# Feature-major inputs, tile-major weights, and a start K tile by K tile, in a one-core hybrid encoder layer

## The chip, the core and the metric

The kernel runs on one core of a Trainium2 chip. The metric is the device time of one execution in microseconds (us). Layout work that the host does on arrays before or after the launch is not in it. Engines: PE is TensorE, DVE VectorE, ACT ScalarE, POOL GpSimd, SP the engine whose queue issues every DMA here.

## What is computed

One layer over 512 prompt tokens and 64 sample tokens, 1,024 features, all float32. Cut to what matters here:

```python
h = rmsnorm(x, norm_mix)                    # over the 1024 features
proj = h @ w_in                             # 1024 x 4104, three head groups
# A: short conv + SiLU, L2-normed q/k, gated delta rule in chunks, gate
# B: differential attention (two softmax maps a head), returns its k and v too
# C: trailing means over 2/4/8/16 frames, a 128x128 map a group
x = x + concat(A, B, C) @ w_out             # 1536 x 1024
u = causal_dwconv(rmsnorm(x, norm_ffn) @ ffn_up)     # 1024 x 5632
x = x + (silu(gate) * value) @ ffn_down     # 2816 x 1024
y = rmsnorm(x, norm_final)
```

Besides y it returns the last rows of every convolution and pooling buffer, attention's keys and values, and the delta-rule states.

## The kernel before

The 576 tokens are the columns of every product and the features its partitions. A product (`gemm`) makes 128 output features: for each of 8 K tiles the weight is split in two float32r parts, `w_hi` (ACT, L177) and `w_lo` (DVE, L178), the activation is in two parts as well, and PE runs hi·hi, hi·lo and lo·hi for token columns 0 to 255 and 256 to 575 (`PARTS`): 48 matmuls of 256 or 320 columns. A weight tile comes through `fetch_weight` (L167, SP queue) into `w_raw`, two buffers; `w_hi` and `w_lo` have two each, and `load_weight` runs one or two products ahead. In `w_in` a weight tile is a set of 128 columns: each row of 512 bytes is a piece of its own, 16,416 bytes from the next.

PE runs in the order of the code: `mm` and `transpose` keep it. One stream of products is woven with chains of small work (`spawn`, `yield` of the expected wait), so a small matmul whose operand is late holds up the products behind it. The other engines' order is set by a scheduler when the program is built.

**Start.** x and the parameters come token-major (`load_rows` L297, `prow`). PE first runs 14 products that nobody reads (`keep_warm`), then transposes x into PSUM, 128x128 at a time (`spread`, 40 transposes, and 4 for the parameters); `split` (L347 on ACT, L348 on DVE) makes the two parts `hmix`, and copies (`xs`) go out to a DRAM tensor `xT_d` (L406), from which the residual is read back (L1154). `first_products` runs the first two products by token part. `rstd1`, the scale of each token, is made meanwhile: squares on ACT, a power on POOL, diagonals `dg` on DVE, and PE spreads them over partitions (`over_tokens`).

**Decay chain.** `decay_products` (32 matmuls with `wab`) follow the first two products; `decays` turns them on DVE, ACT and POOL into `gt` (from `y` L498 to L523), PE sums it, `grow` goes to DRAM (`gsum_d`, L535) and comes back as a broadcast `XT` (L607) for `front`, one head's part of the delta rule: PE transposes k, q and v into PSUM banks, ACT squares and scales them (L610, L628), and PE goes on with `kq` products in the banks that come free.

**Later places.** `blk` (L646, L660) and `inv` (L673, L700) are round trips through DRAM around the 32x32 inversions (L669, L671 on DVE); `levels` (`Xc`, `Y`, `XT`) are small matmuls after them. `token_major` transposes each head's keys and values on PE (10 transposes) and stores both; the cached keys `ckr` are transposed as well (4 a head), and `store_rows` (`rows_out`) transposes six small outputs.

Of the kernel before, what the change touches and what calls it, by code (L numbers as in the profile page):

```python
# [15 lines left out]
P = 128  # L16
# [9 lines left out]
WARM = (10, 0, 4)  # L26
# [33 lines left out]
def hybrid_step(ctx: ExitStack, tc: tile.TileContext, I, O):  # L60
# [10 lines left out]
    # The tensor engine runs in the order of the code.  One stream of products is woven with chains of  # L71
    # smaller work: a chain yields how long its next operands take, and the stream fills that time.
# [61 lines left out]

    def weight_sources():
        for h in range(HEADS):
            for t in (4 + h, h, 8 + h):
                yield [w_in[:, t * P:(t + 1) * P]]
        for base in (1536, 3592):
            for h in range(HEADS):  # L140
                yield [w_in[:, base + h * P:base + (h + 1) * P]]
        for h in range(HEADS):
            for base in (2568, 2056, 3080):
                yield [w_in[:, base + h * P:base + (h + 1) * P]]
        for m in range(KT):
# [25 lines left out]
    def split_weight(raw, step=8):  # L171
# [3 lines left out]
        for a in range(0, kt, step):  # L175
            r = slice(a, min(a + step, kt))
            nc.scalar.copy(hi[:, r], raw[:, r])  # L177
            last_split[0] = nc.vector.tensor_sub(lo[:, r], raw[:, r], hi[:, r].bitcast(F32)).ins  # L178
        return [(hi[:, k], lo[:, k]) for k in range(kt)]
# [8 lines left out]
    def weights():  # L188
        """Those of the next product; the ones after them are set going"""
# [21 lines left out]
    def accumulate(ps, ws, xs, start, stop):  # L211
        """Some K tiles of a product"""
# [7 lines left out]
    def gemm_part(ps, ws, xs, k, r):  # L220
        """What one K tile adds to some columns of a product"""
# [4 lines left out]
    def over_tokens(out, r5, pool, stacked=None):  # L226
        """A number per token (tokens on partitions) to all partitions (tokens on columns)"""
# [18 lines left out]
    # ---------------------------------------------------------------- constants and parameters  # L246
# [25 lines left out]
    xT_d = dram.tile([P, KT, T], F32, name="xT_d")  # L272
# [18 lines left out]
    tiles = ((0, P), (P, P), (2 * P, P), (3 * P, P), (NP, NS))  # L291
    xt = [sp.tile([P, D], F32, name=f"x{t}") for t in range(5)]
    prow = sp.tile([P, 4, P], F32, name="prow")

    def load_rows(t):
        t0, n = tiles[t]
        nc.sync.dma_start(xt[t][:n], I["x_prompt"][t0:t0 + n] if t0 < NP else I["x_sample"])  # L297

    nc.sync.dma_start(ident, I["consts"][:, :P])
    load_rows(0)  # L300
    params = I["params"].rearrange("(g p) c -> p g c", p=P)
    nc.sync.dma_start(prow[:, 0], params[:, 0])
    load_rows(1)
    first_raw = [fetch_weight(), fetch_weight()]
    for t in (2, 3, 4):
        load_rows(t)
    nc.sync.dma_start(prow[:, 1:], params[:, 1:])
    nc.sync.dma_start(wab_raw, w_in[:, 2048:2056].rearrange("(k p) m -> p k m", p=P))
    nc.sync.dma_start(cst[:, P:], I["consts"][:, P:])
# [3 lines left out]
    def keep_warm(n):  # L313
        """Products that nobody reads: the tensor engine's clock halves when it idles"""
# [3 lines left out]
    keep_warm(WARM[0])  # L318
    transpose(pg[:, :P], prow[:, 0], ident)
    nc.vector.tensor_copy(par[:, :P], pg[:, :P])  # L320

    def later_parameters():
        ps = bank()
        for g in range(1, 4):
            transpose(ps[:, g * P:(g + 1) * P], prow[:, g], ident)
        nc.scalar.copy(par[:, P:], ps[:, P:512])

    rstd1 = const.tile([P, T], F32, name="rstd1")
    xs = sp.tile([P, KT, T], F32, name="xs")
# [4 lines left out]
    last_hi, last_lo = [None], [None]  # L334

    def spread(ps, k, ts):
        """Features on partitions"""
        t0 = tiles[ts[0]][0] // CUT * CUT
        for t in ts:
            a, n = tiles[t]  # L340
            transpose(ps[:, a - t0:a - t0 + n], xt[t][:n, k * P:(k + 1) * P], ident[:n, :n])

    def split(ps, k, r):
        """Scaled, in two parts"""
        ps = ps[:, :r.stop - r.start]
        hi, lo = hmix[k]
        last_hi[0] = nc.scalar.activation(hi[:, r], ps, AF.Identity, scale=col("norm_mix", k)).ins  # L347
        last_lo[0] = nc.vector.scalar_tensor_tensor(lo[:, r], ps, col("norm_mix", k), hi[:, r].bitcast(F32),  # L348
                                                    op0=ALU.mult, op1=ALU.subtract).ins

    def mean_square(t):
        n = tiles[t][1]
        junk = sp.tile([P, D], F32, name="junk")
        nc.scalar.activation(junk[:n], xt[t][:n], AF.Square, scale=D ** -0.5, accum_out=r5[:n, t:t + 1])

    def first_products():
        """The first two products begin with the tokens that come first"""
        ra, rb = PARTS
        w = [split_weight(first_raw[0], 4)]
        pair = [bank() for _ in range(4)]  # L360
        for t in (0, 1):
            for k in range(KT):
                spread(pair[k // 2][:, k % 2 * CUT:], k, (t,))
            if t == 0:
                mean_square(0)
                keep_warm(WARM[1])
        keep_warm(WARM[2])
        for k in range(KT):
            split(pair[k // 2][:, k % 2 * CUT:], k, ra)
        with tc.issue_after(last_hi[0]), tc.issue_after(last_lo[0]):  # L370
            w.append(split_weight(first_raw[1], 4))
            for j in range(4):
                src = pair[j].rearrange("p (k t) -> p k t", k=2)
                if j >= 2:
                    with tc.issue_after(last_split[0]):
                        nc.vector.tensor_copy(xs[:, 2 * j:2 * j + 2, ra], src)
                else:
                    nc.scalar.copy(xs[:, 2 * j:2 * j + 2, ra], src)
        ps = [psg.tile([P, 1024], F32, name="g") for _ in range(2)]
        for k in (0, 2, 4, 6, 1, 3, 5, 7):  # L380
            gemm_part(ps[0], w[0], hmix, k, ra)
        rows = {}

        def second(k):
            rows[k] = bank()
            spread(rows[k], k, (2, 3, 4))
            split(rows[k], k, rb)
            if k % 2:
                nc.vector.tensor_copy(xs[:, k, rb], rows[k][:, :rb.stop - rb.start])
            else:  # L390
                nc.scalar.copy(xs[:, k, rb], rows[k][:, :rb.stop - rb.start])

        with tc.issue_after(last_hi[0]):
            for t in range(1, 5):
                mean_square(t)
        rsqrt(r5, r5, EPS)
        scale = over_tokens(rstd1, r5, sp, qscale[:, 4:5])
        for k in range(KT):
            gemm_part(ps[1], w[1], hmix, k, ra)
            if k in (4, 5, 6):  # L400
                second(k - 4)
        for k in range(KT):
            gemm_part(ps[0], w[0], hmix, k, rb)
            if k + 3 < KT:
                second(k + 3)
        nc.sync.dma_start(xT_d, xs)  # L406
        with tc.issue_after(last_lo[0]):
            next(scale)
            nc.vector.tensor_scalar_mul(ah, par[:, oq:oq + 60], 0.5)
        for k in range(KT):  # L410
            gemm_part(ps[1], w[1], hmix, k, rb)
            if k == 1:
                later_parameters()
            if k == 3:
                next(scale, None)
                yield ps[0]
        load_weight()
        yield ps[1]
# [7 lines left out]
    # ---------------------------------------------------------------- small tables  # L426
# [19 lines left out]
    # ---------------------------------------------------------------- decay and beta, token-major  # L446
# [14 lines left out]
    def decay_products():  # L461
# [930 lines left out]
```

## Time and profile before

| | us |
|---|---|
| median of 3 runs | 881.69 |
| lowest and highest run | 881.03, 882.58 |
| span of the profiled execution | 886.6 |
| PE busy in it | 855.8 |
| DVE, ACT, POOL busy | 536.6, 367.1, 112.2 |
| bytes moved by DMA | 87.19 MB, mean 98 GB/s |

The profiled execution has its span alone as its time: 886.6 us from the first to the last instruction, 4.9 us more than the median of the runs. A row of a timeline has the start, the duration, engine, line, operation, out<-in with shapes, how many instructions were merged, and in brackets how long the engine had been idle and what ended that. A float32 matmul of `keep_warm` counts twice (x20 is 10). [...]

### The profile page before, as it was taken

The page shows a single profiled execution, that of the slowest core. Times are in us where ns is not written, and L with a number is a line of the kernel's source. Part 1 is how long each engine was busy: PE and PEld are TensorE (multiplying, and loading weights), DVE is VectorE, ACT ScalarE, POOL GpSimd, SP SyncE. Part 2 cuts the span into 40 slices and gives each one's busy share as a digit, 9 for nine tenths or more (in the row PEclk, how much of TensorE's full clock was granted, in tenths as well). Part 3 has the DMA queues.
Part 4 walks back from the last instruction along what each step waited for, and adds up shares of the span by engine and source line. Part 5 has one row for each costly group of instructions (what it writes and reads, how often), then busy time and mean ns, then how long its engine had stood idle before and what let it go on. Part 6 is the DMA issues. An engine that isn't in the chain of part 4 may idle for free.

```text
span 886.6 us, 16175 instructions
## 1 busy us (share of the span) xinstructions
PE 855.8 (97%) x6422; PEld 825.7 (93%) x6422; DVE 536.6 (61%) x1201; ACT 367.1 (41%) x822; POOL 112.2 (13%) x184
## 2 busy tenths in 40 slices
PE   6997989999999999999999999999999999999996
PEld 6887989898999988888999999999999999999996
DVE  3766866597234667667667677767776774323322
ACT  4535655114345455455445343434343432322322
POOL 0141311031000100000001121212121210000001
PEclk7998999997999999999999999999999999999998
DMA  7635544344333633433752323232323232332412
GB/s 200 168 67 106 61 73 73 69 97 91 63 55 43 145 111 97 122 104 100 258 175 72 96 72 96 73 96 72 95 73 96 72 89 74 113 103 79 121 56 106
DMA packets 144901, 87.19 MB, mean 98 GB/s; under 512 B 10247, under 2 KB 137355, under 8 KB 144699
## 3 DMA queue, kind: packets, MB, share of 16 engines
q1 hardware_dynamic: 144826, 86.17, 38.2%
q8 instruction: 50, 0.82, 0.4%
q14 instruction: 25, 0.20, 0.1%
HBM read 72.98 MB, written 13.17 MB: 97 GB/s over the span
## 4 chain that ended last, share of the span: by engine, by line
PE 82%; DMA 8%; DVE 5%; ACT 2%; issue 1%; POOL 1%; SPq 1%; POOLq 0%; DVEq 0%; ACTq 0%
PE g L85 67%; PE m L85 11%; PE m L89 3%; DMA w_raw<-in_w_in_dram 3%; DVE w_lo L178 1%; DMA w_raw<-in_ffn_down_dram 1%; DVE kq L669 1%; DVE kq L671 1%; DMA gsum_d<-grow 1%; DMA blk<-U 1%; DMA inv<-kq 1%; ACT w_hi L177 1%; DMA XT<-gsum_d 1%; SPq L646 0%; DMA a<-blk 0%
## 5 line engine op out<-in xcount | busy, mean ns | idle before, releaser
L85 PE MATMUL g<-wide,w_hi 128*128 128x256 f32 (+1 forms) x1472 | 277.3, 308 | 7.7 <-ACT w_hi L177 6.4
L85 PE MATMUL g<-t,w_hi 128*128 128x256 f32 (+1 forms) x1408 | 242.7, 294 | 0.0
L85 PEld LDWEIGHTS g<-wide,w_hi 128*128 128x128 f32 x1472 | 230.5, 196 | 12.2 <-ACT w_hi L177 6.8
L85 PEld LDWEIGHTS g<-t,w_hi 128*128 128x128 f32 x1408 | 210.2, 188 | 0.0
L177 ACT CAST w_hi<-w_raw 128x1024 fp32r<-128x1024 f32 (+2 forms) x113 | 112.9, 1000 | 170.1 <-PE g L85 132.1
L85 PE MATMUL g<-wide,w_lo 128*128 128x256 f32 (+1 forms) x736 | 167.9, 307 | 1.2 <-DVE w_lo L178 1.2
L178 DVE TENSOR_TENSOR w_lo<-w_raw,w_hi 128x1024 fp32r<-128x1024 f32 (+2 forms) x113 | 130.7, 1158 | 55.3 <-ACT w_hi L177 54.4
L85 PE MATMUL g<-t,w_lo 128*128 128x256 f32 x704 | 150.4, 295 | 0.0
L85 PEld LDWEIGHTS g<-wide,w_lo 128*128 128x128 f32 x736 | 128.8, 196 | 3.6 <-DVE w_lo L178 1.9
L85 PEld LDWEIGHTS g<-t,w_lo 128*128 128x128 f32 x704 | 117.4, 188 | 0.1
L1275 DVE SCALAR_TENSOR_TENSOR c<-u,par,c 128x511 f32<-128x511 f32 (+3 forms) x176 | 78.9, 511 | 2.5 <-ACT c L1271 2.5
L1278 POOL COPY fout<-u 128x4 f32<-128x4 f32 x44 | 51.1, 1161 | 223.2 <-DVE u L1269 223.2
L1269 DVE TENSOR_TENSOR u<-g,rstd 128x576 f32<-128x576 f32 x44 | 33.3, 758 | 59.8 <-PE g L85 58.3
L85 PE MATMUL g<-w,w_hi 128*128 128x256 f32 (+1 forms) x280 | 48.4, 295 | 0.0
L85 PEld LDWEIGHTS g<-w,w_hi 128*128 128x128 f32 x280 | 42.0, 188 | 0.0
L1271 ACT ACTIVATE c<-u,par 128x576 f32<-128x576 f32 x44 | 38.3, 870 | 4.3 <-DVE u L1269 1.4
L1295 ACT ACTIVATE s<-c 128x576 f32<-128x576 f32 x22 | 15.1, 687 | 46.0 <-DVE c L1277 45.9
L270 POOL TENSOR_TENSOR osc<-sso,mhalf 128x5 f32<-128x5 f32 x8 | 9.3, 1168 | 192.5 <-DVE sso L1030 128.9
L85 PE MATMUL g<-w,w_lo 128*128 128x256 f32 (+1 forms) x140 | 29.9, 295 | 0.0
L1205 ACT ACTIVATE junk<-m 128x128 f32<-128x128 f32 (+1 forms) x40 | 10.8, 273 | 44.2 <-PE m L89 35.9
L1206 DVE TENSOR_TENSOR t<-m,nf 128x128 f32<-128x128 f32 (+1 forms) x40 | 11.2, 289 | 22.6 <-ACT junk L1205 22.6
L998 ACT ACTIVATE p<-m,stat,qscale 128x512 f32<-128x512 f32 (+3 forms) x32 | 19.5, 613 | 12.3 <-DVE stat L995 12.3
(336 smaller groups left out, 1061.4 us busy)
## 6 DMA issues: line engine op xcount, KB each, us to landing
w_raw<-in_ffn_up_dram SPq DMA_DIRECT2D x44, 512.0 KB, 3.9
w_raw<-in_w_in_dram SPq DMA_DIRECT2D x32, 512.0 KB, 8.4
w_raw<-in_ffn_down_dram SPq DMA_DIRECT2D x16, 512.0 KB, 4.0
w_raw<-in_w_out_dram SPq DMA_DIRECT2D x24, 256.0 KB, 3.5
w_raw<-in_ffn_down_dram SPq DMA_DIRECT2D x8, 384.0 KB, 3.3
xT_d<-xs SPq DMA_DIRECT2D x1, 2304.0 KB, 8.0
xr<-xT_d SPq DMA_DIRECT2D x8, 288.0 KB, 3.9
x_d<-xr SPq DMA_DIRECT2D x8, 288.0 KB, 2.5
```

Source lines behind the costliest of these rows:

```text
L85: ordered(nc.tensor.matmul(out, lhsT=lhsT, rhs=rhs, start=start, stop=stop), n / 2.4 if rhs.dtype == F32R else max(54, n / 0.6))
L89: ordered(nc.tensor.transpose(out=out, in_=in_, identity=identity), 107)
L177: nc.scalar.copy(hi[:, r], raw[:, r])
L178: last_split[0] = nc.vector.tensor_sub(lo[:, r], raw[:, r], hi[:, r].bitcast(F32)).ins
L998: nc.scalar.activation(p_m[:, :nk], maps[m], AF.Exp, scale=qscale[:, j:j + 1], bias=st[:, m:m + 1], accum_out=st[:, 2 + m:3 + m])
L1205: nc.scalar.activation(junk[:n], src, AF.Square, scale=D ** -0.5, accum_out=op["part"][:n, c, m:m + 1])
L1206: nc.vector.tensor_mul(op["yt"][c][m // 4][:n, (m % 4) * P:(m % 4 + 1) * P], src, op["nf"][:n, m * P:(m + 1) * P])
L1269: nc.vector.tensor_mul(u, ps[:, O0:O1], rstd)
L1271: nc.scalar.activation(c, u, AF.Identity, scale=fw[:, 2, t:t + 1], bias=col("ffn_conv_b", t))
L1275: nc.vector.scalar_tensor_tensor(c[:, a + d:b], u[:, a:b - d], fw[:, j, t:t + 1], c[:, a + d:b], op0=ALU.mult, op1=ALU.add)
L1278: nc.gpsimd.tensor_copy(fout[:, :, :, t], u[:, NP - 64:].rearrange("p (s c) -> p s c", c=64)[:, :, 62:])
L1295: nc.scalar.activation(s, cv[0], AF.Silu)
```

## The change

The host now hands over x feature-major (`xT`, 128 partitions x 8 K tiles x 576), each weight by output tile (a tile's 8 K tiles lie together on a partition, 4,096 bytes in one piece; `w_out` with its K tiles in the order of use), `cache_k` transposed, and takes keys, conv, pool and ffn rows feature-major. So 86 PE transposes go: 40 of x, 4 of parameters, 20 of keys, 16 of cached keys, 6 of `store_rows`; so do the copies behind them and `xT_d`. Values keep their transposes, y stays token-major.

The first two products go K tile by K tile: weights arrive in K tiles 0 to 1 and 2 to 7, x in four pieces of two K tiles; each K tile is split from SBUF over all 576 columns and both products' matmuls for it follow. The sum of squares is now made on ACT and DVE from the pieces (squared in place) and summed over partitions by PE (`token_sums`, after the decay products), so that `rstd1` starts later. `keep_warm` runs 24 products.

```diff
-WARM = (10, 0, 4)
+WARM = 24
...
             for t in (4 + h, h, 8 + h):
-                yield [w_in[:, t * P:(t + 1) * P]]
+                yield w_in[t]
...
-        kt = 0
-        for src in next(sources):
-            n = src.shape[0] // P
-            nc.sync.dma_start(raw[:, kt:kt + n], src.rearrange("(k p) m -> p k m", p=P))
-            kt += n
+        src = next(sources)
+        kt = src.shape[1]
+        nc.sync.dma_start(raw[:, :kt], src)
         return raw[:, :kt]
...
+    nc.sync.dma_start(par[:, :P], I["params"][:, :P])
+    load_first(slice(0, 2))
+    nc.sync.dma_start(xs[0], I["xT"][:, 0:2])
+    load_first(slice(2, 8))
+    for j in range(1, KT // 2):
+        nc.sync.dma_start(xs[j], I["xT"][:, 2 * j:2 * j + 2])
...
+        for j in range(KT // 2):
+            if j < 2:
+                split_first((slice(0, 2), slice(2, 8))[j])
+            for k in (2 * j, 2 * j + 1):
+                x = xs[j][:, k % 2]
+                hi, lo = hmix[k]
+                nc.scalar.activation(hi, x, AF.Identity, scale=col("norm_mix", k))
+                last_lo[0] = nc.vector.scalar_tensor_tensor(lo, x, col("norm_mix", k), hi.bitcast(F32),
+                                                            op0=ALU.mult, op1=ALU.subtract).ins
+                for w in range(2):
+                    for i, (a, b) in enumerate(((his, hi), (his, lo), (los, hi))):
+                        for r in PARTS:
+                            mm(ps[w][:, O0:O1][:, r], a[w][:, k], b[:, r], start=k + i == 0,
+                               stop=k == KT - 1 and i == 2)
+
+            flat = xs[j].rearrange("p k t -> p (k t)")
+            nc.scalar.activation(flat, flat, AF.Square)
+            sq.append(xs[j])
+            nc.vector.tensor_add(xs[j][:, 0], xs[j][:, 0], xs[j][:, 1])
+            if j:
+                nc.vector.tensor_add(xs[0][:, 0], xs[0][:, 0], xs[j][:, 0])
+        with tc.issue_after(last_lo[0]):
+            nc.vector.tensor_scalar_mul(ah, par[:, oq:oq + 60], 0.5)
+            ab_ps = decay_products()
+        token_sums(xs[0][:, 0], r5)
         scale = over_tokens(rstd1, r5, sp, qscale[:, 4:5])
...
+        next(scale)
         load_weight()
+        next(scale, None)
+        yield ps[0]
+        spawn(decays(decay_rows(ab_ps)), 3250)
+        lambdas()
         yield ps[1]
...
-                nc.sync.dma_start(xr, xT_d[:, m])
+                nc.sync.dma_start(xr, I["xT"][:, m])
```

**What moves, on PE behind the first two products.** Before, `dg,ones` (the scale spread over partitions) stands among the second product's matmuls on the later tokens:

```order
L85 MATMUL g<-wide,w_hi 128x320 x2
L85 MATMUL g<-wide,w_lo 128x320
L85 MATMUL m<-dg,ones 128x128 x4
L85 MATMUL m<-dg,ones 128x64
L85 MATMUL m<-r_129,cst 64x1 x2
L85 MATMUL g<-wide,w_hi 128x320 x2
L85 MATMUL g<-wide,w_lo 128x320
```

Now it stands behind the decay products (`wab`) and right behind the sums over partitions that it is made from:

```order
L85 MATMUL m<-wide,wab 128x320
L85 MATMUL m<-ones,x_92 128x1 x4
L85 MATMUL m<-ones,x_92 64x1
L85 MATMUL m<-dg,ones 128x128 x4
L85 MATMUL m<-dg,ones 128x64
L85 MATMUL m<-r_137,cst 64x1 x2
L85 MATMUL g<-wide,w_hi 128x256
```

No product stands any more between the sums and the scale, nor between the scale and the third product, which takes the PSUM buffer that the scaled first product leaves.

**What moves, on DVE between the decay products and `y`,** the first step of the decay chain (`tmp` is a product times `rstd1`, `kq` the conv of a product, `abT` the scaled decay products). Before:

```order
L473 TENSOR_TENSOR abT<-m,rstd_127 40x256
L473 TENSOR_TENSOR abT<-m,rstd_127 40x320
L578 SCALAR_TENSOR_TENSOR kq<-tmp,ah,kq 128x579
L583 SCALAR_TENSOR_TENSOR kq<-tmp,kq 128x579
L578 SCALAR_TENSOR_TENSOR kq<-tmp,ah,kq 128x579
L498 TENSOR_TENSOR y<-m,vec 128x20
```

Now (the 512-column `tmp` of the first product stands directly ahead of it):

```order
L436 TENSOR_TENSOR abT<-m,rstd_136 40x256
L241 COPY qscale<-m 128x1
L530 TENSOR_TENSOR tmp<-g,rstd_136 128x64
L436 TENSOR_TENSOR abT<-m,rstd_136 40x320
L529 TENSOR_TENSOR tmp<-g,rstd_136 128x512
L530 TENSOR_TENSOR tmp<-g,rstd_136 128x64
L449 TENSOR_SCALAR qneg<-qscale 128x5
L534 SCALAR_TENSOR_TENSOR kq<-tmp,ah,kq 128x579
L450 TENSOR_SCALAR qscale<-qscale 128x5
L534 SCALAR_TENSOR_TENSOR kq<-tmp,ah,kq 128x579 x5
L539 SCALAR_TENSOR_TENSOR kq<-tmp,kq 128x579 x2
L461 TENSOR_TENSOR y<-m,vec 128x20
```

Both convs, eight wide instructions, now stand ahead of `y`; before, three of the eight did between `abT` and `y`, and most of the rest lay ahead of `abT`.

**What moves, on SP's queue at the start.** Now the first issues are:

```order
L298 DMA par<-in_params_dram 128x128
L296 DMA w_raw<-in_w_in_dram 128x256 x2
L300 DMA x_92<-in_xT_dram 128x1152
L296 DMA w_raw<-in_w_in_dram 128x768 x2
L303 DMA x_93<-in_xT_dram 128x1152
L303 DMA x_94<-in_xT_dram 128x1152
L303 DMA x_95<-in_xT_dram 128x1152
```

Two of five x tiles, the identity and the first parameters stood ahead of the first weights; now three quarters of x stand behind them. Behind the start both kernels have the same order on PE up to the inversion, and the same eight weight loads ahead of `gsum_d` and `XT`.

## Rows read from the trace of the kernel before

**Rows 1.** The page's busy times: us, share of the span, instructions.
```profile
PE 855.8 (97%) x6422; PEld 825.7 (93%) x6422; DVE 536.6 (61%) x1201; ACT 367.1 (41%) x822; POOL 112.2 (13%) x184
```
**Rows 2.** Waits: who waited for whom, us in total, times, longest.
```profile
PE m L89 <- ACT kt L610: 2.9, 1, 2.9
PE m L85 <- DVE gt L523: 1.7, 1, 1.7
PE g L85 <- DVE a L1117: 1.3, 1, 1.3
...
PE m L85 <- DMA Xc<-inv: 1.1, 2, 0.7
...
ACT w_hi L177 <- DMA w_raw<-in_w_in_dram: 23.2, 6, 8.0
```
**Rows 3.** Windows: stretch and length, busy by engine (instructions), PEclk, DMA share, GB/s.
```profile
3.00:6.00 3.00, 2.56 (x18) 2.40 (x18) 0.22 (x1) 0.91 (x1) 0.00 (x0) 1.00 0.95 349
9.00:10.50 1.50, 0.00 (x0) 0.00 (x0) 0.58 (x2) 0.00 (x0) 0.00 (x0) 1.00 0.56 74
78.00:84.00 6.00, 6.00 (x26) 5.58 (x27) 5.22 (x11) 2.81 (x10) 0.87 (x3) 0.61 0.55 69
120.00:124.00 4.00, 3.53 (x16) 3.56 (x17) 3.39 (x10) 3.44 (x18) 1.40 (x3) 0.57 0.50 65
210.00:214.00 4.00, 3.44 (x59) 3.03 (x58) 2.54 (x6) 2.79 (x10) 0.00 (x0) 0.50 0.74 126
...
222.00:226.00 4.00, 4.00 (x24) 3.88 (x23) 0.36 (x1) 2.20 (x4) 1.52 (x6) 0.50 0.02 4
```
**Rows 4.** Timeline of PE, start of the program to the third product.
```profile
1.04 3.95 PE L85 MATMUL g<-ones 128*128 128x128 f32 x20 [1.04 <-DVE r L331]
...
7.61 1.06 PE L85 MATMUL g<-ones 128*128 128x128 f32 x8
...
14.89 0.80 PE L85 MATMUL g<-wide,w_hi 128*128 128x256 f32 x2 [6.22 <-ACT w_hi L177]
...
37.87 4.45 PE L85 MATMUL m<-wide,wab 128*128 128x256 f32 x32
...
42.16 0.70 PE L85 MATMUL g<-wide,w_hi 128*128 128x256 f32 x4
```
**Rows 5.** The page's DMA issues: queue, count, KB each, median us to landing.
```profile
w_raw<-in_ffn_up_dram SPq DMA_DIRECT2D x44, 512.0 KB, 3.9
w_raw<-in_w_in_dram SPq DMA_DIRECT2D x32, 512.0 KB, 8.4
```
**Rows 6.** The chain that ended last, 61 to 75 us: start, us, what.
```profile
61.31 7.97 DMA gsum_d<-grow
69.35 5.09 DMA XT<-gsum_d
```
**Rows 7.** Groups by form: count, busy us, mean ns, idle us before them.
```profile
L1260 ACT ACTIVATE t<-w,par 128x576 fp32r<-128x576 f32 x8 | 6.2, 776 | 3.7 <-DVE w L1256 3.7
...
L1261 DVE SCALAR_TENSOR_TENSOR t<-w,par,t 128x576 fp32r<-128x576 f32 x8 | 6.5, 816 | 0.6 <-ACT t L1260 0.5
```
**Rows 8.** Timeline: the later token scale, the decay chain, and `front`'s wait.
```profile
457.20 1.15 PE L85 MATMUL m<-ones,w 128*128 128x1 f32 x10
...
461.85 0.59 ACT L241 COPY rstd<-m 128x512 f32<-128x512 f32 x1 [3.37 <-PE m L85]
...
47.30 0.18 DVE L498 TENSOR_TENSOR y<-m,vec 128x20 f32<-128x20 f32 x1 [1.48 <-PE m L85]
...
58.22 0.62 PE L85 MATMUL m<-gt,cst 128*128 128x20 f32 x4 [1.70 <-DVE gt L523]
...
77.86 1.22 PE L85 MATMUL m<-kq 128*128 128x256 f32 x2 [4.61 <-ACT kt L628]
```
**Rows 9.** Timeline of PE in attention: five transposes of keys, and the product behind them.
```profile
307.68 0.71 PE L89 MATMUL m<-cst,kq 128*128 128x128 f32 x5
308.15 0.77 PE L85 MATMUL g<-wide,w_hi 128*128 128x256 f32 x4
```

More of the change, by code (lines that the diff above doesn't have):

```diff
@@ L174, in split_weight @@
         lo = wp.tile([P, 8, P], F32R, name="w_lo")
[L175 to L178, printed above, removed]
+        nc.scalar.copy(hi[:, :kt], raw)
+        last_split[0] = nc.vector.tensor_sub(lo[:, :kt], raw, hi[:, :kt].bitcast(F32)).ins
         return [(hi[:, k], lo[:, k]) for k in range(kt)]
@@ L290, in hybrid_step, with load_first @@
     sp = startstack.enter_context(tc.tile_pool(name="start", bufs=1, side="right", reuse_waits="tile"))
[L291 to L309, printed above, removed]
+    xs = [sp.tile([P, 2, T], F32, name=f"x{j}") for j in range(KT // 2)]
+    raws = []
+    def load_first(parts):
+        for w in range(2):
+            if len(raws) <= w:
+                raws.append((wp.tile([P, 8, P], F32, name="w_raw"), next(sources)))
+            raw, src = raws[w]
+            nc.sync.dma_start(raw[:, parts], src[:, parts])
+    nc.sync.dma_start(par[:, :P], I["params"][:, :P])
[4 more added lines that the diff above has]
+        nc.sync.dma_start(xs[j], I["xT"][:, 2 * j:2 * j + 2])
+    nc.sync.dma_start(par[:, P:], I["params"][:, P:])
+    nc.sync.dma_start(wab_raw, I["w_ab"])
+    nc.sync.dma_start(cst, I["consts"])
     nc.sync.dma_start(vec, I["vec"].partition_broadcast(P))
@@ L316, in keep_warm @@
             mm(pg[:, 512:640], ones, ones)
[L318 to L326, printed above, removed]
+    keep_warm(WARM)
     rstd1 = const.tile([P, T], F32, name="rstd1")
-    xs = sp.tile([P, KT, T], F32, name="xs")
     r5 = const.tile([P, 5], F32, name="r5")
@@ L333, in hybrid_step @@
     qneg = const.tile([P, 5], F32, name="qneg")
[L334 to L354, printed above, removed]
-    def first_products():
[L358 to L378, printed above, removed]
-        ps = [psg.tile([P, 1024], F32, name="g") for _ in range(2)]
[L380 to L396, printed above, removed]
-        scale = over_tokens(rstd1, r5, sp, qscale[:, 4:5])
[L398 to L416, printed above, removed]
@@ L1185, in token_scale @@
             yield 2550
-            pss = bank()
-            for c in range(5):
-                n = P if c < 4 else NS
-                mm(pss[:n, c:c + 1], sq[:, c * P:c * P + n], ones[:, 0:1])
             r5 = fp.tile([P, 5], F32, name="r5")
             nc.vector.memset(r5, 1.0)
-            nc.vector.tensor_scalar(r5[:, :4], pss[:, :4], 1.0 / D, EPS, op0=ALU.mult, op1=ALU.add)
-            nc.vector.tensor_scalar(r5[:NS, 4:5], pss[:NS, 4:5], 1.0 / D, EPS, op0=ALU.mult, op1=ALU.add)
-            rsqrt(r5, r5)
+            token_sums(sq, r5)
             yield from over_tokens(rstd, r5, fp)
@@ new lines, in _feeds, with _returned, rows @@
+    return {nm: np.ascontiguousarray(a) for nm, a in feeds.items()}
+def _returned(o):
+    def rows(a):
+        return a.transpose(1, 2, 3, 0).reshape(a.shape[1], a.shape[2], -1)
+    conv, pool, ffn = (rows(o[nm]) for nm in ("conv", "pool", "ffn"))
+    k = o["k"].transpose(2, 0, 1)
+    v = o["p_v"].transpose(2, 1, 0, 3).reshape(NP, HEADS, P)
+    out = (o["y_prompt"][None], o["y_sample"][None], o["p_delta"], o["s_delta"], conv[0], conv[1], k[:NP], k[NP:],
+           v, o["s_v"].transpose(1, 0, 2), pool[0], pool[1], ffn[0], ffn[1])
+    return tuple(np.ascontiguousarray(a if i < 2 else a[None, None]) for i, a in enumerate(out))
```

156 lines of the change are left out of this document (78 added, 78 removed).

## The prediction

> **What bounds the kernel now.** I read the busy times first: PE is busy 855.8 of 886.6 us [rows 1], so a PE instruction that goes is worth its time nearly anywhere, and so is a wait of PE; nothing else is. The list of waits then says where PE stood still [rows 2]: besides the 6.2 us at the start, in which the first weights were awaited [rows 4], the stalls are single ones, on `gt`, on ACT's work for a head, on an evacuation, on `Xc`. [...] Last the DMA issues [rows 5]: a 512 KB weight tile of `w_in` took 8.4 us to land, a tile of `ffn_up` of the same size 3.9.
>
> The sum is made on the profiled execution, 886.6 us; it is taken off the median, 881.7, 4.9 lower. A measurement of this kernel tells about 0.2% (1.8 us) from no change.
>
> **Start, to the sums of `gt`: 6.5 us off.** Of the products that nobody reads, ten took 3.95 us and four, later, 1.06 [rows 4]. 24 take 3.95 + 14 x 0.265 = 7.7 from 1.04 on: PE is free at 8.7. Ahead of the first K pair stand 64 KB of parameters, 256 KB of weights and 576 KB of x, 0.92 MB, 2.6 us at the 349 GB/s of the large early loads [rows 3], so they are there by about 5, and hi and lo (0.78 on ACT, 0.82 on DVE [rows 7]) by 7. All of it, 3.47 MB, takes 10 us: by 12 or 13. Per K pair ACT has two hi at 0.78 and a square of twice the width, 3.1; DVE two lo and two additions, at most 4 x 0.82 = 3.3; PE 24 matmuls. A matmul takes 0.134 (32 of them from 37.87 to 42.16 [rows 4]), so 3.2. The three are level and PE begins last: PE sets the pace, and the two products end at 8.7 + 96 x 0.134 = 21.6, the decay products 4.3 later, at 25.9.
>
> Then comes what the new order bares. From the first sum over partitions to the end of the scale's copy took 5.24 us in the feed-forward part (457.20 to 462.44 [rows 8]), there under products; here PE has nothing in between. The scale stands at 31.1, and the first product leaves its PSUM buffer after four DVE instructions: 512 and 256 columns at 0.82 us for 576 [rows 7], two small ones at 0.18 (as `y` [rows 8]), together 1.5. The third product begins at 32.6, where it began at 42.16 [rows 4].
>
> Not all of these 9.6 us last. `y` now stands behind both convs: from 31.1 two instructions of 512 columns, 256 and 320 more, five small ones and eight wide ones at 0.82, 9.8 us, so `y` runs at 40.9 (before at 47.30). From `y` to the sums of `gt` took 10.9 [rows 8], on POOL and DVE, unchanged: 51.8. PE reaches them 14.4 us after the third product's start (58.22 less 1.70 less 42.16), plus 2.3 for a clock lowered by the bare stretch: 49.3. So the wait on `gt` grows from 1.7 to 2.5, and the gain is 58.2 - 51.8 = 6.4, which I round with the rest to 6.5. Bounds: 9 if DVE's chain were no later than PE, 3 if the first loads come 3.5 us later.
>
> **The wait at 77.86: 6.4 off.** Before, `gsum_d` landed after 7.97, `XT` after 5.09, and PE resumed 3.4 later, having waited 4.61 [rows 6, 8]. `gsum_d` is 10 KB; ahead of it in the same queue stands a weight tile. No row has such a tile in pieces of 4 KB. Bounds for `gsum_d`: 7.97 as now, or 3.9, what the tiles of `ffn_up` need whole [rows 5]; I take 3.9, the nearer row, since those are not in shorter pieces than now and `w_in`'s odd row pitch is gone. From 51.8: 3.1 to the issue, 3.9, 5.1, 3.4, so 67.3; PE comes there 15.0 after the sums, at 66.8. 0.5 of 4.61 stays, and the 2.3 of the low clock go. With 7.97 nothing goes.
>
> **The wait at 117: 4.6 off.** ACT stood still for `w_in` tiles for 23.2 us [rows 2]; the last time the squares of a head were behind it in ACT's queue, and PE waited 2.9 for them, 1.7 more by the clock. With tiles in 3.9 there is slack of some 4 us; if they stay at 8.4, nothing goes.
>
> **Smaller waits: 2.4 off.** PE's 1.3 on an evacuation that DVE held behind an inversion waiting for the `blk` round trip, and 1.1 on `Xc` [rows 2]; both are DMA chains beside `w_in` tiles. Either may stay.
>
> **Transposes outside the start: 4.5 off.** Five pushed the next product by 0.47 and its first matmuls by another 0.07 [rows 9], 0.108 each; 20 of keys, 16 of cached keys and 6 of `store_rows` make 42. ACT loses their copies, which nobody awaited. SP issues seven stores fewer, and `xT_d` with its 2.3 MB goes; nobody awaited those. The feed-forward part changes in nothing but its loads, hidden under products there.
>
> Sum: 6.5 + 6.4 + 4.6 + 2.4 + 4.5 = 24.4. 881.7 - 24.4 = **857.3**. Its own range is 851 (`gt` early, every wait gone) to 864 (`gsum_d` as late as now).
>
> **Rivals.**
>
> *Shorter landings do not come.* Pieces of 512 bytes may move as fast as longer ones, and 8.4 be the queue's doing. For it: `ffn_up`'s tiles come in 512-byte pieces too and land in 3.9 [rows 5], so length alone is not what costs. Against it: the same rows say that a tile can land in 3.9 with no shorter queue ahead, and `w_in` differs from `ffn_up` in where its rows lie. Then the waits at 77 and 117 and the smaller ones stay, 13.4 us: 870.7. Chance 0.12. [...]
>
> [...] Each K pair waits for ACT and DVE, and if PE idles between pairs the clock may fall and stay down. 96 matmuls at twice 0.134 end 12.9 later: the first term becomes 6.4 lost, 870.2 in all. Against it: PE is the last of three level engines, so the slower it is the fewer its gaps. Chance 0.08. [...]
>
> *The low clock after the inversion goes.* From 210 to 226 the clock reads 0.50 in four windows of 4 us [rows 3], 8 us lost, begun among the waits on `Xc` and small matmuls. If the waits go, the drop may: 849.3. The small matmuls stay, so 0.12.
>
> *Slower: large pieces land slowly.* At 9 us the DMAs moved 74 GB/s [rows 3]. Should x and the weights come at that, 3.47 MB end at 49, the two products at 53.5, 32 later than I have; `gt` is 25 later than before, the other waits stay, the transposes still go: 902. It is slower than before from a mean below some 130 GB/s (the last pair at 28). Against it: rows of x, 4 KB each, moved at 349 GB/s. Chance 0.03.
>
> **How the numbers follow.** My forecast has 0.60, the rivals 0.12, 0.08, 0.12 and 0.03, mixtures of them 0.05, all faster than before. Faster by over 0.2% is all but the last rival and a sliver: 0.96; within 0.2%: 0.01; slower: 0.03. The range, 848 to 869, holds my own range, the lower rival and the near half of the two at 870; it leaves out under 2 in 10.
>
> **What would show it.** Right: PE's first product near 8.7 and without gaps to 26, at clock 1.00; a bare stretch of about 6.7 us to the third product at 32 to 33; PE at `gt` about 52 after 2 to 3 us of waiting; `w_raw` landing in about 4; no wait on ACT `kt` over 1 us; 36 fewer transposes between 300 and 400. Wrong: tiles that still land in 8, gaps between K pairs, or a new wait in attention, where DVE and ACT have less slack under a shorter stream.

## The result, and the profile after

The changed kernel takes 854.98 us, the median of 4 runs (854.64 to 855.48), against 882.13 (881.03 to 882.80) for the kernel before on the same chip: a ratio of 0.9704, 95% interval 0.9681 to 0.9728. That is 27 us; 24.4 were forecast, 857.3 in all, in a range of 848 to 869. The profiled execution spans 853.0 us. One run below, of ten of the kernel before, took 2,090 us at a clock of 1.00, far off all others, and is left out of the figures.

The page's busy times, which answer to [rows 1]:

```profile
PE 836.9 (98%) x6366; PEld 811.6 (95%) x6366; DVE 536.1 (63%) x1189; ACT 357.1 (42%) x789; POOL 114.5 (13%) x183
```

PE is busy 18.9 us less and stands idle 16.1 us where it stood 30.8. The longest waits of PE, which answer to [rows 2]:

```profile
PE m L85 <- DVE dg L229: 1.9, 1, 1.9
PE m L89 <- ACT p L948: 1.6, 1, 1.6
PE m L85 <- DVE gt L486: 1.4, 1, 1.4
PE g L85 <- DVE tmp L530: 1.1, 1, 1.1
```

The waits on `kt`, on an evacuation and on `Xc` are gone. Those on `dg` and `tmp` come with the new start, the one on `gt` stood at 1.7 before, the one on `p` is new in attention. The windows (columns as in [rows 3]: busy by engine, PEclk, the granted clock as a share of full speed, DMA share, GB/s):

```profile
3.00:6.00 3.00, 3.00 (x23) 3.00 (x23) 0.85 (x2) 0.81 (x2) 0.00 (x0) 1.00 0.92 281
...
27.00:30.00 3.00, 1.11 (x5) 1.12 (x6) 1.32 (x8) 0.00 (x0) 1.19 (x1) 0.69 0.24 96
30.00:36.00 6.00, 4.91 (x24) 4.51 (x24) 4.38 (x12) 2.54 (x4) 1.59 (x6) 0.50 0.01 3
36.00:42.00 6.00, 6.00 (x38) 5.81 (x38) 4.88 (x10) 1.79 (x4) 1.35 (x6) 0.80 0.00 0
60.00:66.00 6.00, 6.00 (x48) 5.95 (x47) 4.48 (x13) 5.56 (x25) 1.73 (x5) 1.00 0.90 235
66.00:72.00 6.00, 6.00 (x44) 5.84 (x44) 5.96 (x16) 3.68 (x11) 1.17 (x4) 1.00 0.30 97
90.00:120.00 30.00, 30.00 (x225) 29.78 (x225) 25.53 (x49) 17.59 (x50) 11.02 (x20) 1.00 0.23 70
180.00:200.00 20.00, 19.95 (x231) 18.95 (x230) 16.25 (x36) 11.97 (x32) 4.12 (x10) 1.00 0.39 107
```

The same instants now belong to other work: the three pieces of work that ran at 0.50 to 0.61 before, at 78, 120 and 210, stand at about 66, 103 and 185 to 200 here and run at 1.00. What is left of the low clock up to 840 us is the bare stretch of the start, from 27 to about 38, and two shorter places behind waits: 0.84 and 0.88 from 48 to 60, at `gt`, and 0.78 and 0.79 from 316 to 324, at `p`. The DMA issues, which answer to [rows 5]:

```profile
w_raw<-in_ffn_up_dram SPq DMA_DIRECT2D x44, 512.0 KB, 3.2
w_raw<-in_w_in_dram SPq DMA_DIRECT2D x30, 512.0 KB, 3.3
```

A tile of `w_in` lands in 3.3 us instead of 8.4. PE's timeline, from the first instruction to `front`, which answers to [rows 4, 8]:

```profile
1.06 7.13 PE L85 MATMUL g<-ones 128*128 128x128 f32 x48 [1.06 <-DVE ones L248]
7.95 0.84 PE L85 MATMUL g<-wide,w_hi 128*128 128x256 f32 x4
...
21.55 4.45 PE L85 MATMUL m<-wide,wab 128*128 128x256 f32 x32
25.83 1.15 PE L85 MATMUL m<-ones,x 128*128 128x1 f32 x10
28.89 2.69 PE L85 MATMUL m<-dg,ones 128*128 128x128 f32 x10 [1.90 <-DVE dg L229]
...
32.98 1.30 PE L85 MATMUL g<-wide,w_hi 128*128 128x256 f32 x4 [1.09 <-DVE tmp L530]
...
51.18 0.62 PE L85 MATMUL m<-gt,cst 128*128 128x20 f32 x4 [1.36 <-DVE gt L486]
...
66.08 0.59 PE L85 MATMUL m<-kq 128*128 128x256 f32 x2
```

The first product begins at 7.95 (forecast 8.7), the products end at 21.55 (21.6), the sums follow at 25.83 (25.9), the third product at 32.98 (32.6), the sums of `gt` at 51.18 (51.8), after a wait of 1.4 (2.5). The second `kq` product, at 66.08 (66.8), which waited 4.61 us before, waits for nothing. Read as rows, the forecast of the start holds to 1 us. What made these rows so is another question, and the experiments answer it otherwise than the forecast did.

### The profile page after: what moved, and what is told of

It reads as the page before. It is cut to its first block, busy times and chain, and to the rows that moved or that the text cites. A ratio compares the mean times of both kernels' runs of the same rounds, so it can differ in the third digit from the quotient of the medians.

```text
span 853.0 us, 15979 instructions
## 1 busy us (share of the span) xinstructions
PE 836.9 (98%) x6366; PEld 811.6 (95%) x6366; DVE 536.1 (63%) x1189; ACT 357.1 (42%) x789; POOL 114.5 (13%) x183
## 2 busy tenths in 40 slices
DMA packets 38888, 84.83 MB, mean 99 GB/s; under 512 B 9370, under 2 KB 14510, under 8 KB 38814
## 4 chain that ended last, share of the span: by engine, by line
PE 95%; DVE 1%; ACT 1%; POOL 1%; DMA 1%; issue 0%; SPq 0%; POOLq 0%; DVEq 0%; ACTq 0%
PE g L85 80%; PE m L85 12%; PE m L89 3%; DMA x<-in_xT_dram 1%; POOL t L477 0%; ACT wide L352 0%; DMA Xc<-inv 0%; POOL t L478 0%; ACT w_hi L341 0%; DVE tmp L529 0%; DVE w_lo L175 0%; POOL r L267 0%; POOL cout L536 0%; ACT x L362 0%; ACT w_hi L174 0%
## 5 line engine op out<-in xcount | busy, mean ns | idle before, releaser
L85 PE MATMUL g<-wide,w_hi 128*128 128x256 f32 x1472 | 268.9, 303 | 1.5 <-DVE tmp L530 1.1
L85 PEld LDWEIGHTS g<-wide,w_hi 128*128 128x128 f32 x1472 | 225.1, 192 | 4.8 <-issue 1.3
L174 ACT CAST w_hi<-w_raw 128x1024 fp32r<-128x1024 f32 (+2 forms) x109 | 110.6, 1015 | 165.5 <-PE g L85 147.3
L85 PE MATMUL g<-wide,w_lo 128*128 128x256 f32 x736 | 161.7, 302 | 0.0
L175 DVE TENSOR_TENSOR w_lo<-w_raw,w_hi 128x1024 fp32r<-128x1024 f32 (+2 forms) x109 | 128.1, 1176 | 44.9 <-ACT w_hi L174 43.9
L85 PEld LDWEIGHTS g<-wide,w_lo 128*128 128x128 f32 x736 | 125.0, 192 | 1.7 <-issue 0.9
L85 PE MATMUL g<-kq,w_hi 128*128 128x256 f32 (+1 forms) x128 | 24.1, 305 | 0.0
```

The lines of the kernel that those rows point to most:

```text
L85: ordered(nc.tensor.matmul(out, lhsT=lhsT, rhs=rhs, start=start, stop=stop), n / 2.4 if rhs.dtype == F32R else max(54, n / 0.6))
L174: nc.scalar.copy(hi[:, :kt], raw)
L175: last_split[0] = nc.vector.tensor_sub(lo[:, :kt], raw, hi[:, :kt].bitcast(F32)).ins
```

## The experiments

### The kernel before, once more

No edit. The forecast rested on one profiled execution, 4.9 us above the median.

> The kernel before, once more, for a second profiled execution. The sum of the prediction was made on one execution of span 886.6 us, 4.9 above the median of the runs, and that one lost 8 us at a clock of 0.50 from 210 to 226. If every execution has that stretch, the spans of these runs lie near 880 with clocks near 0.974 and the excess of the first profile lies elsewhere (the feed-forward part has 1.3 us of waits in it). If the stretch is in some executions alone, the clocks of these runs scatter between 0.974 and 0.985 and the spans by several us with them.

Nine runs went from 877.5 to 886.5 us, median 882.3, ratio to the kernel before 1.0003 (0.9977 to 1.0028); spans from 875.6 to 884.7 with mean clocks from 0.988 to 0.979. So the kernel before scatters by 9 us in nine runs and the changed one by 0.8 in four. Windows of this second profile, span 881.8:

```profile
206.00:210.00 4.00, 3.47 (x45) 3.29 (x46) 3.58 (x9) 3.13 (x8) 2.54 (x4) 0.70 0.67 111
210.00:214.00 4.00, 3.31 (x58) 2.90 (x57) 1.86 (x4) 2.22 (x8) 0.00 (x0) 0.50 0.80 140
214.00:218.00 4.00, 4.00 (x24) 3.72 (x23) 3.30 (x9) 2.83 (x10) 0.00 (x0) 0.52 0.45 75
218.00:222.00 4.00, 4.00 (x42) 3.70 (x40) 3.50 (x8) 2.64 (x7) 1.62 (x4) 1.00 0.00 0
```

The low clock behind the inversion is here too, but ends at 218 instead of 226: busy time times what the clock lacks gives 1.0 + 1.7 + 1.9 = 4.6 us, against 8 in the first profile [rows 3]. That the stretch differs in length between executions makes 3.4 of the 4.8 us between the two profiles. I use both profiles below: us from the span's start to five landmarks (first matmul with `gt`, first with `Xc`, first of the delta scan with `e,kt`, first evacuation `u` of the feed-forward part, end).

| | gt | Xc | scan | u | end |
|---|---|---|---|---|---|
| before, first profile | 58.2 | 207.1 | 247.7 | 462.6 | 886.6 |
| before, second profile | 57.4 | 206.4 | 243.8 | 458.6 | 881.8 |
| before, only `w_in` laid out anew | 51.6 | 185.7 | 218.8 | 433.5 | 856.9 |
| changed, `w_in` in its old rows | 64.5 | 207.9 | 245.5 | 460.3 | 882.5 |
| changed | 51.2 | 184.8 | 217.5 | 431.0 | 853.0 |

### Only the layout of `w_in`, in the kernel before

```diff
-                yield [w_in[:, t * P:(t + 1) * P]]
+                yield [w_in[t]]
...
-            nc.sync.dma_start(raw[:, kt:kt + n], src.rearrange("(k p) m -> p k m", p=P))
+            if len(src.shape) == 2:
+                src = src.rearrange("(k p) m -> p k m", p=P)
+            n = src.shape[1]
+            nc.sync.dma_start(raw[:, kt:kt + n], src)
```

> The kernel before with w_in alone laid out by output tile (4 KB pieces); its start, its transposes and all other layouts stay. My theory: the landings of w_in are what the stalls at 77, 117 and on an evacuation and Xc come from, so w_raw lands in 3.3 to 4 us, those stalls go (6.4, 4.6 and 2.4 us, 13.4 in all), the low clock behind the inversion goes with them where it is there, and the first weights come a little earlier: about 866 us, 860 to 869. Rival one, the new start carries the gain: 876 or more, with a stall near 77 of over 3 us left, since gt is as late as before. Rival two, the landings stay near 8 beside the old stores and round trips: 880.

858.44 us (857.64 to 858.83), ratio 0.9732 (0.9706 to 0.9759): 22.8 us off the 881.22 of the kernel before beside it, more than the 15 that I had expected. The page's row of the tiles, and PE's timeline:

```profile
w_raw<-in_w_in_dram SPq DMA_DIRECT2D x32, 512.0 KB, 3.5
```

```profile
10.63 0.51 PE L85 MATMUL g<-wide,w_hi 128*128 128x256 f32 x2 [0.62 <-ACT w_hi L179]
...
27.87 1.41 PE L85 MATMUL m<-dg,ones 128*128 128x128 f32 x10
...
35.58 0.70 PE L85 MATMUL g<-wide,w_hi 128*128 128x256 f32 x4
...
51.65 0.62 PE L85 MATMUL m<-gt,cst 128*128 128x20 f32 x4 [1.71 <-DVE gt L525]
```

The old start, token-major and with all its transposes, reaches the sums of `gt` at 51.65, the new one at 51.18. Its first product begins at 10.63 instead of 14.89, because the first two tiles are tiles of `w_in` too: the 6.22 us of [rows 4] were the same slow landing. Its third product begins 2.6 us later than the new start's, but it spreads the scale (`dg,ones`, 27.87) under products at full clock (1.00 from 20 to 30). Over the stages, against the second profile: 5.8 us off at the start, 14.9 from there to `Xc`, 4.3 to the scan (the low clock: the windows from 180 to 230 read 1.00), nothing behind. The layout of one input is 24.9 of the 28.8 us between the two spans. For all the rest of the change, the new start and the 86 transposes, 3.9 us are left between the spans, 3.5 between the medians, and the runs of the two kernels do not overlap.

### `w_in` back in its rows, in the changed kernel

```diff
+    w_in_tile = lambda t: w_in[:, t * P + (t >= 16) * 8:][:, :P].rearrange("(k p) m -> p k m", p=P)
...
-                yield w_in[t]
+                yield w_in_tile(t)
...
-        "w_in": tiles(np.concatenate([w_in[:, :2048], w_in[:, 2056:]], 1)),
+        "w_in": w_in,
```

> The changed kernel with w_in alone in its old rows: pieces of 512 bytes, 16,416 bytes from one to the next. The order of all instructions is that of the changed kernel. My theory: w_raw lands in about 8 us again, waits of 3 us or more come back near the first heads, and the time is 855 plus 8 to 20: 863 to 875. Rival, the start and the transposes carried the gain: 859 or less with the landings as slow.

884.28 us, ratio 1.0024 (1.0002 to 1.0045): every microsecond is given back, 9 more than the upper end of what I expected. The waits of PE, and its timeline among the first products:

```profile
PE g L85 <- ACT wide L352: 9.5, 1, 9.5
PE m L85 <- DMA Xc<-inv: 4.5, 2, 4.3
PE m L85 <- ACT kt L584: 2.8, 1, 2.8
```

```profile
12.85 0.42 PE L85 MATMUL g<-wide,w_lo 128*128 128x256 f32 x2
22.79 1.71 PE L85 MATMUL g<-wide,w_hi 128*128 128x256 f32 x4 [9.52 <-ACT wide L352]
24.30 0.68 PE L85 MATMUL g<-wide,w_lo 128*128 128x256 f32 x2
```

With slow tiles the new start is the worse one, by 7.1 us at `gt` (64.5 against 57.4): the larger part of the weights stands ahead of three quarters of x in SP's queue, a piece of x takes 16.7 us to land where it takes 7.3, and PE waits 9.5 us between two K pairs. Behind that wait the products run at half clock (0.68 us for a pair that takes 0.42; the granted clock is 0.50 from 20 to 25). That was the rival of a clock that falls between K pairs, and it shows where the other layout would have left the new order. The changed kernel, at 1.00 from 3 to 27 us, has no such wait.

### Length, alignment, pitch

Five runs change where the bytes of `w_in` lie and nothing else; all instructions keep their order. The pitch is the distance in bytes from the start of one row to the start of the next. Of the edits one is shown, rows padded to 22,528 bytes.

```diff
-        "w_in": tiles(np.concatenate([w_in[:, :2048], w_in[:, 2056:]], 1)),
+        "w_in": np.concatenate([w_in[:, :2048], w_in[:, 2056:], np.zeros((D, 1536), np.float32)], 1),
```

> The same, but rows of w_in padded to 22,528 bytes, those of ffn_up before: pieces of 512 bytes still, now beginning at multiples of 512 bytes. If the odd pitch costs (my theory), w_raw lands in about 4 us as ffn_up did, and the time is 855 to 858. If the length of the pieces costs, it lands in 7 us or more and the time is that of the rows at 16,416. If the traffic beside it is what costs, it lands between the two, near 5 to 6.

> The rows of 22,528 bytes that landed in 3.9 us, with each piece of 512 bytes 32 bytes later, so that none begins at a multiple of 512 bytes; pitch and length stay. Theory one, what costs is where a piece begins: w_raw lands in about 8 us and the time goes to 875 or more. Theory two, the pitch of 16,416 itself costs (rows that fall unevenly on the memory): landing stays near 4 and the time at 855.

> The changed kernel's pieces of 4,096 bytes, also 32 bytes off (each partition's piece 4,128 bytes from the next). Theory: one piece of 4,096 bytes that begins off a multiple of 512 has one ragged begin and end where eight of 512 bytes have eight, so the landing stays near 3.5 us and the time within 2 us of 855. Rival, any misplaced begin slows the whole piece: 6 us or more, 865 or slower.

> The changed kernel with w_in in rows of exactly 16,384 bytes, each piece of 512 bytes at a multiple of 512. A piece that begins 32 bytes off has just cost nothing at 22,528, so theory one is that a pitch near 16,384 itself is what costs (the pieces of a tile all lie nearly 16 KB apart, and fall on the same part of the memory): w_raw lands in 8 us or more and the time is 875 or more. Theory two, only a pitch that is no multiple of 512 costs: it lands in 4 and the time is 855.

> The same with rows of 17,408 bytes, 1,024 more. By theory one (near 16 KB) the landing is 4 us again and the time about 855; should it stay at 8 here too while 22,528 lands in 3.9, the cause is neither alignment nor nearness to 16 KB and stays open.

| `w_in` in the changed kernel | landing | time |
|---|---|---|
| pieces of 4,096 bytes (as changed) | 3.3 | 854.98 |
| the same, 32 bytes off, pitch 4,128 | 3.4 | 854.42 |
| pieces of 512 bytes, pitch 22,528 | 3.9 | 855.81 |
| the same, 32 bytes off | 3.8 | 854.75 |
| 512 bytes, pitch 17,408 | 4.0 | 854.09 |
| 512 bytes, pitch 16,384 | 4.2 | 857.38 |
| 512 bytes, pitch 16,416 (as before) | 7.9 | 884.28 |

The times at 4,128, 17,408, 16,384 and at 22,528 with the offset are of one run each; the ratio at 22,528 is 0.9702 (0.9670 to 0.9734). Two pages' rows of the issues, first of pitch 22,528 with pieces 32 bytes off, then of pitch 16,416, there with the pieces of x:

```profile
w_raw<-in_w_in_dram SPq DMA_DIRECT2D x30, 512.0 KB, 3.8
```

```profile
w_raw<-in_w_in_dram SPq DMA_DIRECT2D x30, 512.0 KB, 7.9
...
x<-in_xT_dram SPq DMA_DIRECT2D x4, 576.0 KB, 16.7
```

Both move their bytes in as many packets, 67,304 (38,888 with the 4 KB pieces). The pages also give the time that the packets of the queue took, as a share of 16 engines' span, first at 22,528, then at 16,416:

```profile
q1 hardware_dynamic: 67230, 83.81, 31.6%
```

```profile
q1 hardware_dynamic: 67230, 83.81, 35.3%
```

Of spans of 854.0 and 882.5 us that is 270 and 312 us for each engine: the same packets and bytes keep the DMA engines busy 42 us longer, so by this figure the packets themselves take longer and do not only wait their turn. The length of the pieces is not what costs: 0.6 us of landing (3.9 against 3.3), no time. A begin 32 bytes off costs nothing (3.8 against 3.9), and a pitch of 16,384, close to the slow one, nearly nothing (4.2). Of the five placements with pieces of 512 bytes only the slow one has a pitch that is no multiple of 512, so that its pieces begin at all multiples of 32 in turn. The 4 KB pieces at a pitch of 4,128 do so too and land in 3.4, so this alone does not cost either: it would have to go together with short pieces. Of the theories above, that a begin off a multiple of 512 costs (pitch 22,528 with the offset) and that a pitch near 16,384 costs (pitch 16,384) both fell; why that pitch costs twice the time stays open. Not tried was a fixed offset other than 32, nor another odd pitch.

### The low clock behind the inversion

```diff
-            yield 6000
+            yield 1500
             for f in pair:
                 U, Xc = f["K"], f["Xc"]
```

> The changed kernel with the small matmuls behind the inversion placed 36 matmuls, some 4.8 us, earlier in the order of PE, so that PE waits about 1.5 to 2.5 us for Xc there, as the kernel before did (0.7 and 0.4 us, more in its second profile); no work is added. Theory, a wait among these small matmuls is what let the clock fall to 0.50 for some 16 us in the kernel before: the clock falls here too, and the time is 859 to 866. Rival, the low clock came from what lay ahead of it (the waits since 170) or the small matmuls of that kernel alone: clock 1.00 but for the wait, 855 to 857.5.

871.12 us, ratio 0.9884 (0.9858 to 0.9911), 16 more than the changed kernel. Windows, and PE's timeline, of this kernel:

```profile
180.00:184.00 4.00, 2.73 (x46) 2.58 (x46) 3.60 (x10) 1.60 (x6) 2.10 (x4) 0.96 0.77 189
184.00:188.00 4.00, 2.39 (x50) 1.97 (x50) 2.91 (x8) 2.37 (x8) 0.00 (x0) 0.50 0.15 23
188.00:192.00 4.00, 4.00 (x24) 3.67 (x20) 2.88 (x8) 2.98 (x10) 0.00 (x0) 0.50 0.01 4
192.00:196.00 4.00, 4.00 (x26) 3.60 (x26) 2.49 (x5) 2.85 (x6) 0.00 (x0) 0.50 0.00 0
196.00:200.00 4.00, 4.00 (x26) 3.88 (x25) 2.62 (x7) 0.76 (x2) 2.29 (x6) 0.50 0.56 187
200.00:204.00 4.00, 4.00 (x74) 3.63 (x73) 0.59 (x2) 0.57 (x2) 0.00 (x0) 0.91 0.02 9
```

```profile
181.10 0.65 PE L85 MATMUL m<-Xc,U 32*32 32x32 f32 x18 [1.71 <-DMA Xc<-inv]
...
187.11 0.47 PE L85 MATMUL m<-Y,XT 32*32 32x32 f32 x5 [1.61 <-ACT XT L660]
```

The clock falls to 0.50 within 3 us of the first wait, and stays there for 16 us, past the second wait and although PE is fully busy from 188 on, as it did in the kernel before. The four windows at 0.50 hold 14.4 us of work, of which 7.2 were lost, and the two waits shown are 3.3. In the changed kernel the same small matmuls stand among equally many products (10, 14 and 6 matmuls between their groups) and run at 1.00, so the waits are what differs. So the theory holds: waits among these small matmuls, which the late landings of `w_in` had caused, cost twice their own length again in clock, 7.2 us behind 3.3. Not every wait does: one of 0.6 us in the same chain, in the kernel with only `w_in` laid out anew (between 190 and 200), left the clock at 1.00. The total is beyond my 859 to 866 for another reason: PE idles 8.6 us between 230 and 420, where it idles 2.6 over the same stretch in the changed kernel (1.00 clock; waits of 2.4 on `stat`, 1.3 on `U`, and more), since the chain that comes earlier also takes its cover of products from others. The whole 16 us are therefore not the price of the low clock.

### The start: the scale under the decay products, and an earlier chain

```diff
+        token_sums(xs[0][:, 0], r5)
+        scale = over_tokens(rstd1, r5, sp, qscale[:, 4:5])
+        next(scale)
         with tc.issue_after(last_lo[0]):
             nc.vector.tensor_scalar_mul(ah, par[:, oq:oq + 60], 0.5)
-            ab_ps = decay_products()
-        token_sums(xs[0][:, 0], r5)
-        scale = over_tokens(rstd1, r5, sp, qscale[:, 4:5])
-        next(scale)
+            ab_ps = decay_products(lambda: next(scale, None))
         load_weight()
-        next(scale, None)
...
         for k in range(KT):
+            if k == 5 and between: between()
```

> The changed kernel with the sums over partitions ahead of the decay products and the spreading of the scale behind five of their eight K tiles, so that the scale is made under them. In the changed kernel the sums' input was there at 21.1 us, the sums ran at 25.83 and the third product began at 32.98, at half clock until 38. Now: sums at 21.6, dg by 25, scale by 27.3, third product at 28.7 at full clock. My theory: 4.3 us earlier there, and gt, 19.5 us behind the scale, by 47, with PE waiting some 3.7 for it, so that 3 to 4.4 us of it last: 851, 850 to 853. Rival, DVE's w_lo work (1.18 us each) gets between and PE waits for dg as long as before: 854 to 855.

857.13 us (854.89 to 858.37), ratio 0.9727 (0.9698 to 0.9757): no gain. DVE's timeline in this kernel:

```profile
34.60 0.17 DVE L461 TENSOR_TENSOR y<-m,vec 128x20 f32<-128x20 f32 x1
...
47.12 1.22 DVE L175 TENSOR_TENSOR w_lo<-w_raw,w_hi 128x1024 fp32r<-128x1024 f32 x1
48.25 0.17 DVE L483 SCALAR_TENSOR_TENSOR gt<-t,ea 128x20 f32<-128x20 f32 x1
...
49.22 0.06 DVE L486 MEMSET gt<- 64x4 f32 x1
```

The third product did begin at 29.27 and the clock stayed at 1.00 to 46, but `gt` was there only at 49.3, 1.8 us earlier: `y` came 6.0 earlier, and then its chain's small steps, the last ones above all, stood behind wide instructions of the conv and `w_lo` on DVE, 14.6 us from `y` to `gt` instead of the 10.5 in the changed kernel. PE waited 5.7 us for it, its clock fell to 0.53, and 2.4 more went on ACT's `kt`. What I named a rival, DVE's order, did decide, but at `gt`, not at `dg`. So the bare stretch was not what bound the start: the decay chain was.

The next edit comes on top of this one:

```diff
-        spawn(decays(decay_rows(ab_ps)), 3250)
...
+        chain = decays(decay_rows(ab_ps))
+        spawn(chain, next(chain) + 3500)
         yield ps[0]
```

> The same, and the decay chain begins directly behind the decay products instead of behind both convs: y should run near 32 instead of 40.6, gt be there by 43, and PE reach its sums near 43 without a wait over 1 us. My theory: 51.2 less 43 is 8 us: 847, 846 to 850. Rival, the first stall moves on: front's transposes wait for XT or for the convs, which DVE now does later, and no more than early_sums' gain is left: 851 or more.

849.91 us (849.62 to 851.71), ratio 0.9645 (0.9620 to 0.9670): 5.1 us below the changed kernel's median, with an interval that lies below that kernel's own. PE's timeline:

```profile
46.15 0.59 PE L85 MATMUL m<-gt,cst 128*128 128x20 f32 x4 [1.79 <-DVE gt L487]
...
61.37 0.70 PE L85 MATMUL m<-kq 128*128 128x256 f32 x2 [1.69 <-ACT kt L585]
```

`gt`'s sums run 5.0 us earlier than in the changed kernel and the end comes 4.8 earlier (848.2): the gain at this point lasts to the end, since PE is bound from there on. It is 3 us short of what I expected, as `y` at 31.98 still needed 14 us to `gt`. So, on top of both edits, the polynomial went from POOL to DVE, and the sums of `gt` were placed earlier among PE's products, since the chain was to be shorter:

```diff
-        spawn(chain, next(chain) + 3500)
+        spawn(chain, next(chain) + 2000)
...
-        nc.vector.tensor_scalar(t1, z2, 1.0 / 17, 1.0 / 15, op0=ALU.mult, op1=ALU.add)
-        for d in (13, 11, 9, 7, 5, 3, 1):
-            nc.gpsimd.tensor_mul(t1, t1, z2)
-            nc.gpsimd.tensor_scalar_add(t1, t1, 1.0 / d)
+        nc.vector.tensor_scalar_mul(t1, z2, 1.0 / 17)
+        for d in (15, 13, 11, 9, 7, 5, 3):
+            nc.vector.scalar_tensor_tensor(t1, t1, 1.0 / d, z2, op0=ALU.add, op1=ALU.mult)
```

> The kernel with the early decay chain, and the polynomial of that chain written for DVE (8 instructions of 0.18 us) instead of 14 small ones on POOL that take 8.2 us; the same terms, in another form of the same sum. gt was there at 45.9 and PE waited 1.8 for it; now some wide DVE instructions get between, so gt at 43 to 44 with PE there at 43. Theory: the stall at gt goes and 2 us with it: 848, 847 to 850. Rival, PE is bound next by XT's round trip and by ACT's copies for the first head (1.7 us in that kernel), so that nothing is gained: 849.5 to 851.

849.56 us (849.25 to 853.58), ratio 0.9653 (0.9629 to 0.9678): no different from the kernel with POOL's polynomial. PE's timeline:

```profile
44.29 0.59 PE L85 MATMUL m<-gt,cst 128*128 128x20 f32 x4 [1.24 <-DVE gt L487]
...
56.43 0.33 PE L89 MATMUL m<-cst,kq 128*128 128x128 f32 x1 [1.35 <-ACT kt L567]
```

The sums of `gt` ran 1.9 us earlier, still after a wait of 1.2, and PE then waited for ACT's squares of the first head; the rival was right.

## Why the prediction was right, and where not

**Start, 6.5 forecast; 7.0 in the first profile's rows, 6.2 in the second's.** Every instant of the sum came out to within 1 us, yet the term was credited to the wrong cause, so that its size was right by luck. The step that failed is the comparison itself: I set the new order against the old start as it stood with slow tiles, [rows 4], and put its 6.22 us wait down to the old order. The old start with fast tiles is at `gt` within 0.5 us of the new one (51.65 against 51.18); with slow tiles the new order loses 7.1. The order K tile by K tile is thus worth about half a microsecond here, the landing some 6.

**The waits at 77 and 117 and the smaller ones, 13.4 forecast; 15.3 between `gt` and `Xc`.** Right in place and nearly in size. `gsum_d` was issued at 54.2 and `XT` at 57.6, so it landed in under 3.4 where I took 3.9; no wait is left at 66.08, where I had left 0.5. Of the two reasons that I gave for short landings, the pitch was the right one, and only the runs show it: with 512-byte pieces at another pitch the gain is the same. The 2.3 and 1.7 for the low clock behind the two waits are what 0.61 lacks over the 6 us from 78 and 0.57 over the 4 us from 120 [rows 3]; the second profile of the kernel before reads 0.72 and 0.50 there. That the bare stretch of the start would cost the same 2.3 was an estimate: busy time times what the clock lacks gives 4.0 in the windows from 27 to 42.

**Transposes, 4.5 forecast; about 2.6 measured,** 1.2 from the scan to the feed-forward part and 1.4 behind, against the kernel with only `w_in` changed. The step left out what I named as a possible mistake: a new wait in attention, 1.6 us on ACT's `p`, with the clock at 0.78 and 0.79 in the windows from 316 to 324 around it, which lost 1.5. Together with the 1.2 these 3.1 are 4.3, near the 3.9 that the 36 transposes of keys would give at 0.108. That the wait comes from slack that is missing under a shorter stream was not tried by itself. Of the 1.4 behind, a wait of 0.5 on `w_lo` and two transposes are seen in the rows, the rest is not traced.

**The low clock behind the inversion, 8, as a rival with a chance of 0.12.** It came true: 7.9 us between `Xc` and the scan by the first profile, 4.7 by the second. I had put the drop down to the small matmuls, which stay. In the changed kernel they run at 1.00, and with waits among them at 0.50: it was the waits, which were already on my list of those that go. So what came is the main forecast and this rival together, a mixture, which I gave 0.05 with all others. The chance should have been that of the waits' going.

**Shorter landings do not come, 0.12, and large pieces land slowly, 0.03:** both wrong, 3.3 us. **The first products at half clock, 0.08:** no, the clock was 1.00 from 3 to 27, with one wait of 0.3 us between K tiles; but it is what the same code does when tiles are slow, behind a wait of 9.5 us, with 0.50 from 20 to 25.

The sum of 24.4 stands against 33.6 between the profiles first compared, 28.8 with the second profile of before, and 27.1 between medians. The excess is mostly the clock, and the transposes take some back. That the point forecast was only 2.3 us high is in part luck: the clock was missing from the sum, while the sum, made on a profile with 3.4 us more of the low clock than the next one, was taken off the median. The lower end of my own range, 851, does not follow from its terms: with `gt` early (9 for 6.5) and every wait gone (0.5 more) they give 27.4 off, 854.3, just under the median measured.

## What to carry to other kernels

When one kind of transfer takes twice as long as another of its size, look at the pitch of its rows: here padding them to another pitch (884.3 to 855.8 us) gave what pieces of eight times the length gave. Before crediting a rewrite of a stage, ask what the old stage would do with the other half of the change; one run with that half alone tells. A wait of PE among small matmuls is to be priced with the clock behind it, which here cost 7.2 us behind waits of 3.3, and nothing behind one of 0.6.

## What the runs showed of the hardware that was not expected

A pitch of 16,416 bytes doubled the landing of 512-byte pieces (7.9 us against 3.8 to 4.2 at 16,384, 17,408 and 22,528, there also 32 bytes off), and slowed what stood behind in the queue as well: pieces of x took 16.7 us instead of 7.3.

In the run with the chain placed earlier the clock, once at 0.50 among matmuls of 32x32, stayed there through 12 us in which PE was busy in the profile throughout (188 to 200), and rose only about 200; in the kernel before it rose at 226 in one execution and at 218 in another. The kernel before scattered over 9 us, the changed one over 0.8; that this comes from the length of such stretches fits the spans and clocks of its runs, and was not tried.
